# A larger pad at the top of SBUF: right-hand MLP operands 256 bytes off the weights, where they were 128 off

## The chip, the cores and the metric

The kernel runs on one core of one Trainium2 chip. The metric is the device time of one execution in microseconds; less is better. The time before is the median of three runs.

## The reference

One decoder layer on `x` of 1 x 1024 x 1024, all in float32: a mixer block, an MLP block and a final RMSNorm. Cut to what matters here:

```python
for l in range(DEPTH):                                   # DEPTH = 1
    h = rms_norm(x, norm_mix[l])
    x = x + hybrid_mixer(h, ...)                         # 8 projections 1024->1024, RG-LRU, HGRN2, gates, w_out
    h = rms_norm(x, norm_mlp[l])
    x = x + jnp.square(jax.nn.relu(h @ w_up[l])) @ w_down[l]   # 1024 -> 4096 -> 1024
return rms_norm(x, norm_final)
```

The MLP block is where the change acts.

## The kernel before, in words

**How a float32 product is made.** Every large matrix operand is split into a high part (a rounding to TensorE's `fp32r` type) and a low part (what is left), each a tile of its own. `split` writes them, ScalarE the high part (L76) and VectorE the low part (L77). `mm3` then makes one product from three matmuls, L115, L116 and L117:

```python
def mm3(o, ah, al, bh, bl, first, last, goes_on=False):
    PE.matmul(o, ah, bh, start=first, stop=False, **how)    # L115
    PE.matmul(o, ah, bl, start=False, stop=False, **how)    # L116
    PE.matmul(o, al, bh, start=False, stop=last, **how)     # L117
```

The first operand of a matmul (`ah`, `al`) is the one loaded into the array, 128 columns or 512 bytes of a partition; below it is called the loaded operand. The second (`bh`, `bl`) is streamed, 512 columns or 2048 bytes of a partition (256 columns in `pv` alone); below it is called the streamed operand. Each matmul has a weight load of its own, and TensorE loads the operand of the next matmul while the present one streams.

**The stages.** First the mixer, in two halves of the sequence: projections (`pj_*`, `pv`), the recurrences, gates, and the output projection (`po`). Then the second norm, made while the second half's output projection runs. Then the *up* stage (`hidden`, matmuls `uX`, `uY`, `uZ`), 16 quads of hidden channels with a seven-product scheme (`PLAN`): 16 x 7 x 4 x 3 = 1344 matmuls of 512 columns. Its squared-ReLU results are split and, for 14 of 16 quads, written to DRAM. Last the *down* stage (`dX`, `dY`, `dZ`), eight blocks of two quads each, again 1344 matmuls, added into `acc` by VectorE (L963), then the final norm and the output. The scheduler's order on every engine is fixed when the kernel is built.

**Where the operands lie.** Tiles are taken from a stack that grows from the left (low addresses) and one that grows from the right (the top of SBUF, downward). On the left lie, among others, the raw and split weights (`wp`: `wH`, `wL`, `ws..`, `wA..`; `w1`), the mixer's activations (`a2h`: `hT`, `a2y`: `y`), and the first set of MLP hidden operands (`ust`: `u0..`, `u2..`). All of these start at 256 past a multiple of 512 bytes. On the right lie the up stage's streamed operands (`h2..`), and in the down stage a second set of everything (`late_u`, `late_w`, `late_w1`, `late_raw`) and the sums `acc`. Ahead of all of these stands a tile that nobody uses:

```python
pad, close_pad = opened("pad", side="right")
pad.tile([P, 24], F32, tag="pad", name="pad")            # 96 bytes of a partition
h2p = [opened(f"h2{i}", side="right") for i in range(4)]
```

All tiles behind it are multiples of 512 bytes long, so the pad alone sets where each of them starts, modulo 512: before, at 384. Within the tiles every slice that a matmul of these stages takes starts at a multiple of 512 bytes. So, modulo 512:

| | loaded operand | streamed operand |
|---|---|---|
| projections `pj`, output projection `po` | 256 (`wH`, `wL`) or 256 (`y`) | 256 (`hT`) or 256 (`wH`, `wL`) |
| up stage `uX`, `uY`, `uZ` | 256 (`ws`, `wA`) | 384 (`h2..`) |
| down stage, first quad of a block | 256 (`ust`) | 256 (`wp`, `w1`) |
| down stage, second quad of a block | 384 (`late_u`) | 384 (`late_w`, `late_w1`) |

In the down stage the two quads take turns:

```python
for i, q in enumerate(qs):                               # i = 0: left tiles, i = 1: right tiles
    for pr in prs:
        mm3(banks[bk, pr], uh[:, cut], ul[:, cut], wh, wl, ...)
```

With two `pr` that is six matmuls with left tiles, then six with right tiles. So at the last matmul of each six the streamed operand lies on one side, and the next operand, loaded meanwhile, on the other.

Of the kernel before, what the change touches and what calls it, by code (L numbers as in the profile page):

```python
# [10 lines left out]
F32 = mybir.dt.float32  # L11
# [7 lines left out]
P = 128  # L19
# [22 lines left out]
def trunk(ctx: ExitStack, tc: tile.TileContext, x, wts, mlp, pv, gains, mask_f, mask_u, out):  # L42
# [8 lines left out]
    def opened(name, **how):  # L51
        cm = tc.tile_pool(name=name, bufs=1, reuse_waits="tile", **how)
        return cm.__enter__(), lambda: cm.__exit__(None, None, None)
# [617 lines left out]


    pad, close_pad = opened("pad", side="right")
    pad.tile([P, 24], F32, tag="pad", name="pad")

    h2p = [opened(f"h2{i}", side="right") for i in range(4)]
    HOME = {"T4": 0, "B22": 0, "T3": 0, "B21": 1, "n2": 2, "t1": 2, "B11": 3}
# [371 lines left out]
```

## Time and profile before

| | |
|---|---|
| median of 3 runs | 1626.46 us (1626.07 to 1626.98) |
| the profiled execution, its own time | 1627.6 us |
| its span, first to last instruction | 1625.8 us |
| mean granted TensorE clock | 0.996 |
| up stage, first to last matmul in the trace | about 987 to 1309 us |
| down stage | about 1304 to 1618 us |

The time differs from the span by 1.8 us, which lies outside the instructions. "Busy" counts an engine's instructions, without waits. A matmul's record is longer than the time until the next one starts, since matmuls overlap in the array: a record of 0.39 us stands in a row of starts that are 0.23 us apart. The pace of TensorE is therefore read from the starts, or from a stretch of time over the number of matmuls in it. Releasers (what ended a wait) are inferred.

### The profile page before, as it was taken

Reading aid. Unit: us, or ns where it says so; the run is one execution under the profiler, and the core shown is the slowest. Engines: PE = TensorE matmul, PEld = TensorE weight load, DVE = VectorE, ACT = ScalarE, POOL = GpSimd, SP = SyncE. Lnnn points to the kernel's source line nnn. Section 1 sums busy time; section 2 is a strip of 40 time slices with the busy share of each in tenths; the row PEclk is TensorE's granted clock in tenths of the full one; section 3 lists DMA queues with packets and bytes.
Section 4 is the critical chain, followed back from the end, with each engine's and each line's share of the span. In section 5 each row is a group of like instructions: output and inputs, shape, how many; then the busy total and the mean of one; then the engine's idle time right before and its main releaser. Section 6 shows DMA issues by size and latency. Waiting matters only on the chain.

```text
span 1625.8 us, 23177 instructions
## 1 busy us (share of the span) xinstructions
PE 1583.0 (97%) x9240; PEld 1306.5 (80%) x9240; DVE 1212.2 (75%) x1751; ACT 764.6 (47%) x1186; POOL 65.0 (4%) x99
## 2 busy tenths in 40 slices
PE   7999999999999999999999997999999999999998
PEld 6788788788788788788787876888888877888886
DVE  5975956848764865848759688977777888788876
ACT  4643545435442544436434566766776732222113
POOL 0010100100100000000100100000000000000000
PEclk9999999999999999999999998999999999999999
DMA  6212212122243222222122362666656575666652
GB/s 237 91 66 91 92 66 104 66 91 92 79 167 135 86 78 90 80 78 103 67 91 91 117 207 104 248 248 250 237 233 246 223 269 213 256 255 247 256 209 104
DMA packets 57996, 246.51 MB, mean 152 GB/s; under 512 B 6688, under 2 KB 6816, under 8 KB 47136
## 3 DMA queue, kind: packets, MB, share of 16 engines
q1 hardware_dynamic: 56304, 239.27, 39.4%
q10 hardware_dynamic: 1584, 5.77, 1.0%
q8 instruction: 72, 1.18, 0.3%
q14 instruction: 36, 0.29, 0.1%
HBM read 185.24 MB, written 59.77 MB: 151 GB/s over the span
## 4 chain that ended last, share of the span: by engine, by line
PE 80%; DVE 15%; DMA 2%; issue 1%; ACT 1%; POOL 0%; DVEq 0%; POOLq 0%; SPq 0%; ACTq 0%
PE uX L115 3%; PE uX L117 3%; PE dX L115 3%; PE uX L116 3%; PE dX L117 3%; PE dX L116 3%; DVE wL L77 2%; PE pj_ga L117 2%; PE pv L116 2%; PE pv L117 2%; PE pv L115 2%; PE pj_ga L115 2%; PE pj_ga L116 2%; PE pj_f L117 2%; PE pj_ma L115 2%; PE pj_ma L117 2%
## 5 line engine op out<-in xcount | busy, mean ns | idle before, releaser
L77 DVE TENSOR_TENSOR wL<-raw,wH 128x1024 fp32r<-128x1024 f32 x160 | 194.3, 1214 | 150.0 <-ACT wH L76 145.8
L76 ACT CAST wH<-raw 128x1024 fp32r<-128x1024 f32 x160 | 167.8, 1049 | 166.3 <-issue 66.4
L963 DVE TENSOR_TENSOR acc<-acc,dX 128x512 f32<-128x512 f32 x128 | 85.1, 682 | 30.4 <-PE dX L117 29.7
L76 ACT CAST wA<-q 128x512 fp32r<-128x512 f32 x32 | 19.8, 621 | 129.0 <-PE dX L117 102.1
L963 DVE TENSOR_TENSOR acc<-acc,dY 128x512 f32<-128x512 f32 x64 | 43.5, 685 | 16.0 <-PE dY L117 15.1
L345 DVE RECIPROCAL rr<-rr 128x512 f32<-128x512 f32 x16 | 53.5, 3346 | 0.0
L823 ACT ACTIVATE b<-b 128x512 f32<-128x512 f32 x48 | 30.2, 631 | 38.4 <-DVE b L822 38.3
L115 PE MATMUL pv<-wH,hT0H 128*128 128x256 f32 x128 | 37.7, 294 | 0.0
L116 PE MATMUL pv<-wL,hT0H 128*128 128x256 f32 x128 | 37.4, 293 | 0.0
L117 PE MATMUL pv<-wH,hT0L 128*128 128x256 f32 x128 | 37.4, 292 | 0.0
L115 PE MATMUL pv<-wH,hT1H 128*128 128x256 f32 x128 | 36.5, 285 | 0.0
L116 PE MATMUL pv<-wL,hT1H 128*128 128x256 f32 x128 | 36.2, 283 | 0.0
L117 PE MATMUL pv<-wH,hT1L 128*128 128x256 f32 x128 | 36.2, 283 | 0.0
L311 DVE SCALAR_TENSOR_TENSOR xc<-xp,pvt,xc 128x512 f32<-128x512 f32 x48 | 33.1, 746 | 0.0
L551 ACT ACTIVATE on<-po 128x128 f32<-128x128 f32 x64 | 17.0, 278 | 33.4 <-PE po L541 33.2
L570 ACT ACTIVATE smb<-pj_mb 128x512 f32<-128x512 f32 x16 | 9.6, 597 | 45.4 <-PE pj_mb L117 45.2
L824 ACT ACTIVATE b<-b 128x512 f32<-128x512 f32 x48 | 30.0, 630 | 1.1
L77 DVE TENSOR_TENSOR wA<-q,wA 128x512 fp32r<-128x512 f32 x32 | 21.9, 686 | 10.5 <-ACT wA L76 10.3
L565 ACT ACTIVATE g<-pj_g 128x512 f32<-128x512 f32 x16 | 9.6, 599 | 37.3 <-PE pj_g L117 37.3
L444 POOL TENSOR_SCALAR seg<-seg 128x128 f32<-128x128 f32 (+1 forms) x16 | 12.7, 792 | 360.4 <-DVE seg L384 360.4
L384 DVE TENSOR_TENSOR seg<-seg 128x128 f32<-128x128 f32 (+2 forms) x96 | 26.7, 305 | 0.2
L117 PE MATMUL pj_ga<-hT1H,wL 128*128 128x512 f32 x64 | 26.5, 414 | 0.0
(1854 smaller groups left out, 5264.3 us busy)
## 6 DMA issues: line engine op xcount, KB each, us to landing
raw<-wts_in SPq DMA_DIRECT2D x160, 512.0 KB, 3.4
q<-mlp_in SPq DMA_DIRECT2D x64, 512.0 KB, 4.0
x<-x_in SPq DMA_DIRECT2D x8, 512.0 KB, 5.8
acc<-x ACTq DMA_DIRECT2D x8, 512.0 KB, 6.5
y_out<-acc SPq DMA_DIRECT2D x16, 256.0 KB, 2.1
xs<-x_in SPq DMA_DIRECT2D x8, 256.0 KB, 3.3
x<-xs SPq DMA_DIRECT2D x8, 256.0 KB, 2.4
x2s<-x_in SPq DMA_DIRECT2D x4, 512.0 KB, 4.4
```

What stands on the lines that cost most here:

```text
L76: keep(A.copy(h, src))
L77: keep(V.tensor_tensor(out=lo, in0=src, in1=h.bitcast(F32), op=ALU.subtract))
L115: PE.matmul(o, ah, bh, start=first, stop=False, **how)
L116: PE.matmul(o, ah, bl, start=False, stop=False, **how)
L117: PE.matmul(o, al, bh, start=False, stop=last, **how)
L311: V.scalar_tensor_tensor(xc[:, s, :], xp[:, j : j + T], pvt[:, PV_CW + 8 * j + u : PV_CW + 8 * j + u + 1], xc[:, s, :], op0=ALU.mult, op1= ...
L345: V.reciprocal(rec, rec)
L384: mul = lambda o, a, b: V.tensor_tensor(out=o, in0=a, in1=b, op=ALU.mult)
L551: A.activation(on[:, 4 * s + n, :], po[:, n * P : (n + 1) * P], AF.Square, accum_out=ssq[:, 4 * s + n : 4 * s + n + 1])
L823: A.activation(b[:, at, :], b[:, at, :], AF.Relu, scale=-1.0 if at == 2 else 1.0)
L824: A.activation(b[:, at, :], b[:, at, :], AF.Square)
L963: V.tensor_tensor(out=dst, in0=dst, in1=banks[bk, pr], op=op)
```

## The change

The unused tile at the top of SBUF is 480 bytes of a partition long in place of 96. Every tile of the right-hand stack that comes after it (`h2..`, `late_u`, `late_w`, `late_w1`, `late_raw`, `acc`) lies 384 bytes lower, and so starts at a multiple of 512 bytes, where it started at 384 past one. Nothing on the left moves, and the instructions, their order and their waits stay the same on every engine.

```diff
     pad, close_pad = opened("pad", side="right")
-    pad.tile([P, 24], F32, tag="pad", name="pad")
+    pad.tile([P, 120], F32, tag="pad", name="pad")
 
     h2p = [opened(f"h2{i}", side="right") for i in range(4)]
```

In the table above each 384 becomes 0 (or 512); the 256 stay.

## The prediction

> **What bounds the kernel now.** I read the page first, for the bound; then the starts of matmuls in three stages, for TensorE's pace; then who makes TensorE wait in the two stages that the change touches.
>
> ```profile
> span 1625.8 us, 23177 instructions
> PE 1583.0 (97%) x9240; PEld 1306.5 (80%) x9240; DVE 1212.2 (75%) x1751; ACT 764.6 (47%) x1186; POOL 65.0 (4%) x99
> PE 80%; DVE 15%; DMA 2%; issue 1%; ACT 1%; POOL 0%; DVEq 0%; POOLq 0%; SPq 0%; ACTq 0%
> 1100.00:1200.00 100.00, 100.00 (x431) 80.31 (x430) 78.98 (x97) 69.63 (x97) 0.00 (x0) 1.00 0.61 237
> 1400.00:1500.00 100.00, 100.00 (x440) 82.54 (x439) 78.68 (x113) 20.16 (x22) 0.00 (x0) 1.00 0.57 226
> PE uX L115 <- ACT ws30H L76: 1.7, 1, 1.7
> PE uZ L115 <- ACT braw L705: 0.5, 1, 0.5
> PE dZ L116 <- DVE wA1230L L77: 1.1, 1, 1.1
> PE dX L115 <- DVE acc L963: 1.1, 3, 0.4
> ```
>
> The last six rows are two stretches of the view by windows (busy time and count of TensorE, its weight loads, VectorE, ScalarE, GpSimd; then granted clock, share of the DMA engines, GB/s) and all that the view of waits lists for TensorE from 990 us to the end; the row above them is the chain that ended last, four fifths of it TensorE. In the up stage (1100 to 1200) and the down stage (1400 to 1500) TensorE is busy all the time at full clock, VectorE under 80%, and in 636 us it waits 4.4 us. So there the time is the number of matmuls times the distance of their starts, and only what alters that distance counts.
>
> That distance is not the same everywhere. Here are the first and last row of three unbroken stretches of TensorE's instructions in order of time (start, us, line, out<-streamed,loaded for `pj` and `u`): 84 rows of a projection, 100 of the up stage, 103 of the down stage.
>
> ```profile
> 644.77 0.39 PE L115 MATMUL pj_f<-hT1H,wH 128*128 128x512 f32 x1
> ...
> 663.58 0.39 PE L117 MATMUL pj_g<-hT1H,wL 128*128 128x512 f32 x1
> 1134.82 0.40 PE L117 MATMUL uY<-h2t1H,ws17L 128*128 128x512 f32 x1
> ...
> 1157.92 0.39 PE L117 MATMUL uX<-h2n2H,ws18L 128*128 128x512 f32 x1
> 1469.71 0.39 PE L117 MATMUL dX<-ws122H,u6n 128*128 128x512 f32 x1
> ...
> 1492.98 0.39 PE L117 MATMUL dZ<-wA1223H,u7B 128*128 128x512 f32 x1
> ```
>
> Projection: (663.58 - 644.77) / 83 steps = 226.6 ns. Up stage: (1157.92 - 1134.82) / 99 = 233.3 ns here, and over the longer window 100 us / (431 - 1.7) = 232.9 ns (a record of 0.39 us begins up to 1.7 steps before the window and is counted in it). Down stage: (1492.98 - 1469.71) / 102 = 228.1 ns. Same kind of matmul, same shape, same clock. In the table of addresses they differ in one thing: in the projection the streamed operand and the operand being loaded have the same place modulo 512, in the up stage they lie 128 apart, in the down stage 128 apart once in six matmuls.
>
> That it is the address and not the stage is seen at the turns of the down stage:
>
> ```profile
> 1440.25 0.40 PE L117 MATMUL dY<-ws320H,u4B 128*128 128x512 f32 x1
> 1440.48 0.39 PE L115 MATMUL dY<-ws321H,u5B 128*128 128x512 f32 x1
> 1440.71 0.39 PE L116 MATMUL dY<-ws321L,u5B 128*128 128x512 f32 x1
> 1440.94 0.39 PE L117 MATMUL dY<-ws321H,u5B 128*128 128x512 f32 x1
> 1441.17 0.39 PE L115 MATMUL dY<-ws321H,u5B 128*128 128x512 f32 x1
> 1441.39 0.39 PE L116 MATMUL dY<-ws321L,u5B 128*128 128x512 f32 x1
> 1441.62 0.40 PE L117 MATMUL dY<-ws321H,u5B 128*128 128x512 f32 x1
> ```
>
> The two matmuls of 0.40 us, first and last, are the ones that stream from one side while the next operand is loaded from the other; the five between, with both on the right, are shorter. And it does not matter which way: in the first the streamed operand lies at 256 and the loaded one at 384, in the last at 384 and 256. A loss that is the same at +128 and at -128 is the second fact on which I build.
>
> **The change, part by part.** *The up stage.* The offset between streamed and loaded goes from 128 to 256 (modulo 512) for 1344 matmuls. No matmul of 512 columns in this trace has that offset, so its price is bounded from both sides. From below, the best pace in the trace, 226.6 ns at offset 0: a gain of 232.9 - 226.6 = 6.3 ns a matmul. From above, a loss that grows with the distance: offset 128 costs 6.3 ns over offset 0, so 256 would cost 12.6, that is 6.3 ns more than now. The middle is the same price as now.
>
> I take the lower end. If two streams disturb each other by meeting in the same part of a memory that repeats every 512 bytes, one that runs ahead by 128 and one that runs behind by 128 (ahead by 384) meet at different times of the load, and I'd expect different losses. If the pattern repeats every 256 bytes, +128 and -128 are the same offset, as the two equal rows have it. Then 256 is the same as 0. One other place has an offset of 256, in matmuls of 128 columns in the mixer (`sn` at 384 is streamed while `scT` at 128 is loaded; `v` at 128 while `qf` at 256):
>
> ```profile
> 425.49 0.38 PE L541 MATMUL po<-sn,qf 128*128 128x128 f32 x2
> 425.71 0.39 PE L538 MATMUL po<-v,scT 128*128 128x128 f32 x2
> 425.93 0.39 PE L541 MATMUL po<-sn,qf 128*128 128x128 f32 x2
> 426.15 0.39 PE L538 MATMUL po<-v,scT 128*128 128x128 f32 x2
> ```
>
> Each pair starts 0.22 us after the one before, whether it ends with an offset of 256 (L541) or of 128 (L538). So 256 brings no loss of its own there; but 128 brings none either, so this speaks only weakly.
>
> Some 1300 of the 1344 matmuls gain, since the first dozens wait for others (the two `ws30H` and `braw` rows above). 1300 x 6.3 ns = 8.2 us. Nothing else holds that stage: VectorE has 79 us of work in 100 us, and it would have it in 97.3. Only the stage's end is different, as the chain that ended last shows:
>
> ```profile
> 1286.95 1.05 ACT wA1215H L76
> ...
> 1303.64 4.62 DMA q<-mlp_in
> ...
> 1311.72 1.15 DVE wA1230L L77
> 1312.91 0.50 PE dZ L116
> ```
>
> From 1287 to 1313 it runs through ScalarE, VectorE and a load of weights and not through TensorE. What TensorE gains in those 26 us, 26 x 6.3 / 232.9 = 0.7 us, it waits out at `dZ` L116, on top of the 1.1 us there now. Left of the up stage: 7.5 us.
>
> *The down stage.* Within a quad both operands move together or neither moves: no change. At the turns the offset goes from 128 to 256, in both directions. By the paces above the turns now cost 228.1 - 226.6 = 1.5 ns a matmul on average, 1344 x 1.5 = 2.0 us. If 256 is as 0, that goes; TensorE waits for little there, so I count 1.9 us of it.
>
> *Everything else on the right.* VectorE and ScalarE read and write there, and DMAs land there. VectorE shows no price for an offset: the split into `h2T3L` reads one operand at 256 and one at 384, that into `wA` two at 256:
>
> ```profile
> L77 DVE TENSOR_TENSOR h2T3L<-braw,h2T3H 128x512 fp32r<-128x512 f32 x2 | 1.4, 688 | 0.0
> L77 DVE TENSOR_TENSOR wA<-q,wA 128x512 fp32r<-128x512 f32 x17 | 11.6, 685 | 0.2
> ```
>
> 3 ns either way on the few hundred VectorE instructions of these stages is under 1 us, and it lies under TensorE with a fifth of VectorE's time free; without that cover it would be that 1 us. DMAs into right-hand tiles are covered the same way: of the waits in the down stage none is long and only the chain above has a load in it. I count nothing for both.
>
> Sum: 7.5 + 1.9 = 9.4 us. The profiled execution took 1627.6 us (span 1625.8), so it would take 1618.2; the median of the runs is 1.1 us lower, which gives 1626.5 - 9.4 = 1617.1 us.
>
> **The rule that speaks against it.** TensorE's pace depends on where the operands lie, 226.6 against 232.9 ns. The Trainium skill, "TensorE: Matmul & The Clock Gate", Part 2 (what happens when a matmul is issued), has two independent SBUF read ports in TensorE, and says that loading the next tile's weights takes no read bandwidth from the running matmul. By that rule no offset would matter, and the time would stay at 1626.5 us. The two paces above don't agree with it, as long as nothing but the offset tells the stages apart; the 0.40 us rows inside one stage are my reason to think so.
>
> **The rivals.** *Not faster, not slower.* A load and a stream may disturb each other once for every time that one overtakes the other, at a fixed price whenever that falls inside the load, so that only offset 0, where they start together, escapes. Equal rows at +128 and -128 fit this too. Then 256 costs what 128 costs: 1626.5 us. The case in which offsets mean nothing at all, and the stages differ by something that I haven't seen, ends at the same time. Against both: a meeting early and a meeting late in the load should leave a different rest of the load to suffer.
>
> *Slower.* The loss grows with the distance, and 256, half way round 512, is the farthest that two operands can be apart: the meeting falls in the middle of the load, where most of it is still to come or just done. It also is the same at +128 and -128, so the two rows can't exclude it. Priced linearly: 1300 x 6.3 = 8.2 us in the up stage, 2.0 us at the turns, 1636.7 us. It decides once the up stage's starts are more than 235.3 ns apart: 0.2% of the time is 3.25 us, over 1344 matmuls 2.4 ns each, on 232.9.
>
> *Part of the gain.* 256 is better than 128 but not as good as 0, or the end of the up stage and the first loads of the down stage hold back more than 0.7 us: half the sum, 1621.8 us.
>
> **How the numbers follow.** About 0.2%, 3.25 us, is what a measurement of this kernel can tell from no change. Faster as summed: 0.51; part of it: 0.08; no change: 0.15; slower: 0.26. So faster 0.59, same 0.15, slower 0.26. The likeliest case's own range is 1615 (the whole 8.5 us of 1344 matmuls, the turns, and 1 us for matmuls that may go below 226.6) to 1620. Cases of both signs hold most of the chance, so the full range runs from 1614 past no change into the slower case, up to 1634, three quarters of its linear price; its far end, and the little below 1614, are left out with less than 2 in 10.
>
> **What would show it.** In the profile after: starts in the up stage 226.6 to 227.5 ns apart, that is 441 to 443 matmuls in a window of 100 us in which 431 stood; no 0.40 us rows at the turns of the down stage, and 442 or 443 there in place of 440; the wait at `dZ` L116 grown from 1.1 to about 1.8 us; projections and everything before 980 us as before; VectorE's 688 and 685 ns unchanged. I am wrong if the up stage keeps 431 (rival of no change) or shows under 427 (slower), and wrong in the reason if the time falls elsewhere.

## The result: 0.41% faster

| | median | runs |
|---|---|---|
| before | 1626.35 us | 6 (1625.81 to 1627.95) |
| after | 1619.25 us | 6 (1618.30 to 1622.63) |

The ratio is 0.9959, with a 95% interval of 0.9946 to 0.9972: 6.7 us, between 4.6 and 8.8. The profiled execution after took 1621.54 us with a span of 1619.7, 6.1 us under the span before. The forecast was 1617.1 us.

The page after; the view by windows for TensorE alone (window, length, busy time and count, clock, DMA share, GB/s); and, in order of time, the first and the last of 103 unbroken rows of the up stage and of 104 of the down stage:

```profile
span 1619.7 us, 23177 instructions
PE 1574.4 (97%) x9240; PEld 1304.5 (81%) x9240; DVE 1211.2 (75%) x1751; ACT 763.1 (47%) x1186; POOL 64.9 (4%) x99
PE 77%; DVE 17%; DMA 2%; issue 2%; ACT 1%; POOL 0%; DVEq 0%; POOLq 0%; SPq 0%; ACTq 0%
```

```profile
1100.00:1200.00 100.00, 99.66 (x438) 1.00 0.62 240
1210.00:1280.00 70.00, 70.00 (x309) 1.00 0.64 248
1510.00:1600.00 90.00, 90.00 (x398) 1.00 0.44 174
```

```profile
1134.69 0.39 PE L115 MATMUL uY<-h2t1H,ws17H 128*128 128x512 f32 x1
...
1157.81 0.39 PE L115 MATMUL uZ<-h2B21H,wA128H 128*128 128x512 f32 x1
...
1469.42 0.39 PE L117 MATMUL dZ<-wA1223H,u7B 128*128 128x512 f32 x1
...
1492.77 0.39 PE L115 MATMUL dY<-ws323H,u7B 128*128 128x512 f32 x1
```

Up stage: 23.12 us / 102 steps = 226.7 ns, where it was 233.3. Down stage: 23.35 / 103 = 226.7 ns, where it was 228.1. Both now have the projection's pace. The turns of the down stage, which stood out with 0.40 us, are gone. The rows below pass from the left tiles (`u4B`) to the right ones (`u5B`) between 1440.86 and 1441.09:

```profile
1440.63 0.39 PE L116 MATMUL dX<-wA,u4B 128*128 128x512 f32 x1
1440.86 0.39 PE L117 MATMUL dX<-wA,u4B 128*128 128x512 f32 x1
1441.09 0.39 PE L115 MATMUL dX<-wA,u5B 128*128 128x512 f32 x1
```

So in unbroken rows every matmul got what was forecast. The window from 1100 to 1200 us holds 438 matmuls all the same, and not the 441 to 443 of the forecast, because TensorE pauses in it. Here is all that the view of waits lists for TensorE from 985 to 1310 us, the second norm's (`xT_h`) left out:

```profile
PE uX L115 <- ACT ws30H L76: 2.0, 1, 2.0
PE uZ L115 <- ACT braw L705: 1.1, 1, 1.1
PE dZ L116 <- DVE wA1230L L77: 0.9, 1, 0.9
PE uX L117 <- DVE wA L77: 0.5, 1, 0.5
...
PE uX L115 <- ACT e L819: 0.3, 1, 0.3
```

Before, the first two were 1.7 and 0.5 us, and the last two weren't there; the one at `dZ`, which lies behind 1310 us there, was 1.1. In the up stage proper TensorE waits 3.9 us where it waited 2.2. Not all of these waits cost time; the part on the sum below says which do.

### The profile page after: what moved, and what is told of

Same layout as the page of the kernel before. It is cut to its first block, busy times and chain, and to the rows that moved or that the text cites. A ratio compares the mean times of both kernels' runs of the same rounds, so it can differ in the third digit from the quotient of the medians.

```text
span 1619.7 us, 23177 instructions
## 1 busy us (share of the span) xinstructions
PE 1574.4 (97%) x9240; PEld 1304.5 (81%) x9240; DVE 1211.2 (75%) x1751; ACT 763.1 (47%) x1186; POOL 64.9 (4%) x99
## 4 chain that ended last, share of the span: by engine, by line
PE 77%; DVE 17%; DMA 2%; issue 2%; ACT 1%; POOL 0%; DVEq 0%; POOLq 0%; SPq 0%; ACTq 0%
PE dX L115 3%; PE dX L116 3%; PE dX L117 3%; PE uX L115 3%; PE uX L117 3%; PE uX L116 3%; DVE wL L77 2%; PE pj_ga L117 2%; PE pv L116 2%; PE pv L117 2%; PE pv L115 2%; PE pj_ga L116 2%; PE pj_ga L115 2%; PE pj_f L117 2%; PE pj_ma L117 2%; PE pj_ma L116 2%
## 5 line engine op out<-in xcount | busy, mean ns | idle before, releaser
L116 PE MATMUL pv<-wL,hT0H 128*128 128x256 f32 x128 | 37.5, 293 | 0.0
L116 PE MATMUL pv<-wL,hT1H 128*128 128x256 f32 x128 | 36.2, 283 | 0.0
```

## The experiments

Two theories stood against each other at first. Mine: the price of an offset between streamed and loaded operand repeats every 256 bytes. The rivals: it grows with the distance, or only offset 0 escapes; or what counts is an address by itself, not the offset. The runs below change a pad and nothing else. For each I show the two windows that measure the pace: with c matmuls in 70 us of the up stage a step is 70 / (c - 1.7), with c in 90 us of the down stage 90 / (c - 1.7). Short pauses in a window are counted in. One matmul more or less is 0.8 and 0.6 ns. Before the change they hold:

```profile
1210.00:1280.00 70.00, 70.00 (x302) 1.00 0.60 234
1510.00:1600.00 90.00, 90.00 (x396) 1.00 0.46 181
```

That is 233.1 and 228.3 ns. After it (309 and 398, above) 227.8 and 227.1 ns. The up stage's 227.8 has two short gaps in it, at an operand `ws3..` of every second quad.

### Offset 0

```diff
-    pad.tile([P, 24], F32, tag="pad", name="pad")
+    pad.tile([P, 56], F32, tag="pad", name="pad")
```

> Pad of 224 bytes: the right-hand operands at 256 modulo 512, as the weights, offset 0. If the pattern repeats every 256 bytes, offset 0 is as 256: up stage 226.6 to 227.1 ns from start to start, time 1618 to 1620 us, as with the pad of 480. If the loss grows with the distance up to some point and 256 is merely a better place than 128, offset 0 is better still: up stage under 226 ns, 1617 us or less. If 256 is a place of its own and 0 is not, up stage near 230 ns, over 1622 us.

```profile
1210.00:1280.00 70.00, 70.00 (x309) 1.00 0.67 257
1510.00:1600.00 90.00, 90.00 (x398) 1.00 0.44 172
```

1618.73 us, ratio 0.9949 (0.9934 to 0.9963). The same counts as with offset 256, to the matmul. The first theory holds so far; 256 is no mere way-point between 128 and something better.

### Offset -128

```diff
-    pad.tile([P, 24], F32, tag="pad", name="pad")
+    pad.tile([P, 88], F32, tag="pad", name="pad")
```

> Pad of 352 bytes: the right-hand operands at 128 modulo 512, 128 below the weights in place of above. If the pattern repeats every 256 bytes, -128 is the same offset as +128: up stage 232.8 ns, turns of the down stage costing 1.5 ns a matmul, 1626.4 us as before. If what counts is which stream is ahead, the up stage has another pace, under 230 or over 236 ns, and the time is more than 3 us away from before.

```profile
1210.00:1280.00 70.00, 70.00 (x302) 1.00 0.61 233
1510.00:1600.00 90.00, 90.00 (x396) 1.00 0.48 189
```

1627.04 us, ratio 1.0001 (0.9991 to 1.0010). Again the counts of +128 exactly. What the turns of the down stage hinted at holds over the whole up stage.

### The weights moved in place of the operands

```diff
+    const.tile([P, 32], F32, tag="padl", name="padl")
     ident = const.tile([P, P], F32, tag="ident", name="ident")
```

This stands on the kernel before, with its pad of 96 bytes; the unused tile comes ahead of `ident`.

> Pad of 96 bytes on the right as before, and an unused tile of 128 bytes at the bottom on the left, so that the weights and all else on the left lie at 384 modulo 512, as the right does: the streamed operands of the up stage keep their addresses modulo 512, and the offset becomes 0. If the offset between the two counts, up stage 227 ns, turns at the common pace, 1618 to 1620 us. If it is the address of the right-hand tiles by itself that counts (384 bad, 0, 256 and the like good), nothing is gained: 232.8 ns, 1626.5 us, and the mixer, whose operands now lie at 384 too, gets slower than 226.6 ns as well.

```profile
1210.00:1280.00 70.00, 70.00 (x309) 1.00 0.67 257
1510.00:1600.00 90.00, 90.00 (x398) 1.00 0.44 172
```

1619.46 us, ratio 0.9953 (0.9935 to 0.9971). The right-hand tiles lie where they lay before, at 384, and the gain is there all the same; with the larger pad the weights lay where they lay before, at 256, and it was there too. So it is the offset between the two operands, and not where either lies.

### The up stage alone, and the down stage alone

```diff
+    pad2, close_pad2 = opened("pad2", side="right")
+    pad2.tile([P, 32], F32, tag="pad2", name="pad2")
     late_u, close_late_u = opened("late_u", side="right")
```

That is the up stage alone, on the kernel after; `pad2` is also closed at the end with the other tiles. The down stage alone has the pad of 96 bytes and `pad2` of `[P, 96]`.

> Pad of 480 bytes for the up stage, and a second pad of 128 bytes that puts everything of the down stage on the right back to 384 modulo 512, as before. By the prediction's terms the up stage keeps its gain and the turns of the down stage lose theirs: up stage 227.0 ns, down stage 228.1 ns, about 2 us slower than the pad of 480 alone (1620.5 to 1621.5 us). If the down stage's gain came from something else on the right (landing DMAs, VectorE), it goes too, and the matmuls with both operands on one side would be seen to change.

> Pad of 96 bytes for the up stage as before, and a second pad of 384 bytes that puts the down stage's right-hand tiles at multiples of 512. The other half of the run with the up stage alone: up stage 232.8 ns as before, turns of the down stage at the common pace, about 2 us under before: 1624 to 1625 us. If the gains of the two stages don't add (the down stage's first loads holding back), it is under 1 us.

Up stage alone:

```profile
1210.00:1280.00 70.00, 70.00 (x309) 1.00 0.65 250
1510.00:1600.00 90.00, 90.00 (x396) 1.00 0.44 172
```

Down stage alone:

```profile
1210.00:1280.00 70.00, 70.00 (x302) 1.00 0.61 233
1510.00:1600.00 90.00, 90.00 (x399) 1.00 0.47 182
```

1620.95 us, ratio 0.9963 (0.9950 to 0.9976), and 1625.50 us, ratio 0.9985 (0.9976 to 0.9995). Each stage keeps its own pace, gained or not, whatever the other does. The two gains, 6.0 and 2.4 us by the ratios, add up to 8.4, which the whole change's own interval of 4.6 to 8.8 us holds. The down stage has only its turns to gain from, so these are worth about 2 us, as summed.

### Smaller offsets: +64, -64, -32, +32

```diff
-    pad.tile([P, 24], F32, tag="pad", name="pad")
+    pad.tile([P, 40], F32, tag="pad", name="pad")
```

That is offset 64. `[P, 8]` gives 192, `[P, 128]` 224 and `[P, 48]` 32. By a period of 256 bytes 192 is -64 and 224 is -32.

> Pad of 160 bytes: offset 64. If a loss rises smoothly from offset 0 to its height at 128, 64 lies between: up stage about 230 ns, 1622 us. If two streams disturb each other wherever they are not exactly in step (offset 0 modulo 256), 64 costs what 128 costs: 232 to 234 ns, 1626 us. If parts of memory of 128 bytes take turns, 64 is half in the same part and half in the next, 228 to 232 ns.

> Pad of 32 bytes: offset 192, which by a period of 256 is -64. The run at +64 had 229.1 ns in the up stage and 230.7 ns within the quads of the down stage, 1626.0 us in all; at its turns the streams at -64 were followed by starts 227.2 ns apart, those at +64 by 230.9. If the sign counts below 128, the up stage at -64 is faster than at +64: 226 to 228 ns. If it is only the distance, 229 ns. The whole then 1618 to 1626 us, since the turns of the down stage have both signs in either case.

> Pad of 512 bytes, which modulo 512 is no pad at all: offset 224, by a period of 256 that is -32. If the loss is smooth round 0, under 1 ns a matmul: 1619 to 1621 us. If any step out of a common multiple of 128 or 64 costs, 229 ns and more, 1622 to 1628 us.

> Pad of 192 bytes: offset +32, the mirror of the run at 224 (-32), which had 233.3 ns in the up stage. If the sign counts as it does at 64 (229.1 ns at +64, 233.3 at -64), +32 lies well below 233, 227 to 230 ns. If only in step (0 modulo 256) is free and +64 is the exception, 232 to 234 ns. The whole 1622 to 1628 us, since the turns of the down stage have both signs.

Offset 64:

```profile
1210.00:1280.00 70.00, 70.00 (x306) 1.00 0.63 242
1510.00:1600.00 90.00, 90.00 (x392) 1.00 0.44 175
```

Offset 192, or -64:

```profile
1210.00:1280.00 70.00, 70.00 (x302) 1.00 0.61 233
1510.00:1600.00 90.00, 90.00 (x393) 1.00 0.47 185
```

Offset 224, or -32 (modulo 512 the place that the tiles have without a pad):

```profile
1210.00:1280.00 70.00, 70.00 (x301) 1.00 0.61 233
1510.00:1600.00 90.00, 90.00 (x393) 1.00 0.47 184
```

Offset 32:

```profile
1210.00:1280.00 70.00, 70.00 (x301) 1.00 0.60 232
1510.00:1600.00 90.00, 90.00 (x393) 1.00 0.46 180
```

| offset | up stage, ns | down stage, ns | median, us | ratio (interval) |
|---|---|---|---|---|
| +64 | 230.0 | 230.6 | 1625.98 | 0.9992 (0.9982 to 1.0001) |
| -64 | 233.1 | 230.0 | 1629.64 | 1.0019 (1.0010 to 1.0029) |
| -32 | 233.9 | 230.0 | 1629.10 | 1.0008 (0.9999 to 1.0018) |
| +32 | 233.9 | 230.0 | 1629.27 | 1.0012 (1.0003 to 1.0021) |

Here my expectations mostly missed. At +64 the up stage came out half way, as a smooth curve would have it, but the time didn't. At -64 I had read from a few turns that it would be fast, and it is as slow as 128: what follows a single turn doesn't tell the pace of a row of such matmuls. At 32, either way, the loss is as large as at 128. So the price is no smooth function of the distance. Of the eight offsets tried it is gone only at 0 and 256; +64 is the one place between.

The down stage shows a second thing. Within a quad both operands lie alike, and still it runs at 230.0 to 230.6 ns with turns of 32 or 64, slower than with turns of 128 (228.3). At offset 64 the records show where:

```profile
1441.56 0.40 PE L117 MATMUL dX<-wA1221H,u5t 128*128 128x512 f32 x1
1441.79 0.40 PE L115 MATMUL dX<-wA1221H,u5t 128*128 128x512 f32 x1
1442.03 0.39 PE L116 MATMUL dX<-wA1221L,u5t 128*128 128x512 f32 x1
1442.25 0.39 PE L117 MATMUL dX<-wA1221H,u5t 128*128 128x512 f32 x1
1442.48 0.39 PE L115 MATMUL dX<-wA,u4B 128*128 128x512 f32 x1
1442.71 0.40 PE L116 MATMUL dX<-wA,u4B 128*128 128x512 f32 x1
```

The turns are at 1442.25 and, ahead of these rows, at 1440.88. The long records are the third and fourth matmul after the one and the second after the other, among operands that are in step. It is no chance of these rows: over the 82 unbroken groups of six that follow a turn like the first of these, the third and the fourth matmul take 233.1 and 235.5 ns to the next start. So the loss doesn't stay with the matmul at the turn. The kernel before has a little of it too: 232.5 ns at the turn and 230.6 at the matmul behind it, and 226 to 227 at the other four.

### Offsets 256 and 0, side by side

The two kernels of before, unchanged, in five rounds on one chip.

> The changed kernel itself once more (pad of 480, offset 256), beside the pad of 224 (offset 0) on the same chip. If the two offsets are one and the same, the medians lie within 1 us of each other, near 1619 us, and the up stage runs at 227.0 ns in both. The 2 us that were short of the forecast: if they go to a stretch of half clock after the first wait of the up stage that some executions have and some have not, single times fall into two groups about 1.6 us and more apart, the lower near 1618.3.

> Pad of 224 bytes (offset 0) again, beside the pad of 480. Same as the pad of 480 if the period is 256: within 1 us. If 256 has a price of its own that its profile hid (the mean of the starts is then over 0.4 ns apart), this one is faster by 1 us or more.

Offset 256: 1619.34 us (1617.76 to 1620.91), ratio 0.9950 (0.9937 to 0.9962). Offset 0: 1618.96 us (1618.29 to 1619.86), ratio 0.9948 (0.9935 to 0.9960). They are the same within what can be told; no version of these beats the changed kernel. The two groups of times that I expected don't show: 1617.76, 1619.09, 1619.34, 1619.95 and 1620.91 lie too evenly. But the first profile of the changed kernel has a stretch of half clock in this window, and this second one has not. Window 1005 to 1020 us (TensorE, its weight loads, VectorE, ScalarE, GpSimd, clock, DMA) and some rows in it, the first execution:

```profile
1005.00:1020.00 15.00, 12.97 (x49) 9.92 (x48) 7.29 (x11) 7.93 (x14) 0.00 (x0) 0.89 0.19 70
```

```profile
1010.33 0.50 PE L115 MATMUL uX<-h2T3H,ws30H 128*128 128x512 f32 x1 [1.97 <-ACT ws30H L76]
...
1013.23 0.63 PE L115 MATMUL uX<-h2T3H,ws30H 128*128 128x512 f32 x1
1013.65 0.63 PE L116 MATMUL uX<-h2T3L,ws30H 128*128 128x512 f32 x1
1014.08 0.63 PE L117 MATMUL uX<-h2T3H,ws30L 128*128 128x512 f32 x1
```

and the second:

```profile
1005.00:1020.00 15.00, 12.98 (x57) 10.08 (x56) 8.90 (x13) 9.49 (x17) 0.00 (x0) 1.00 0.19 70
```

In the first, eight matmuls after the 2 us wait start 0.43 us apart in place of 0.23, at a mean clock of 0.89 over the window. That is 8 x 0.20 = 1.6 us, and the two profiled executions are 1621.54 and 1619.09 us long. From 1011.9 to 1015.3 us the granted clock is 0.50 in the first and 1.00 in the second. The same stretch stands in five of the 13 profiles: with the up stage in step (this one and the up stage alone) and out of step (offsets 64 and -128, the down stage alone). So the change doesn't bring it about.

## Why the prediction was right

**The bound and the pace.** Right: starts 226.7 ns apart in both stages, 226.6 was the forecast.

**The price of 256.** Right, and for the reason given: 0 and 256 are one offset, +128 and -128 another, in whole stages and not only at the turns. The rival in which only offset 0 escapes needed 302 matmuls in the window and there are 309. The rival in which the loss grows with the distance falls with 32, which costs as much as 128, and with 256, which costs nothing. Some luck was in it: the step from two equal rows at the turns to a period of 256 is the kind of reading that failed at -64. And what it is that repeats every 256 bytes stays open; the runs show the price, not its cause.

**The rule on the read ports.** The Trainium skill, "TensorE: Matmul & The Clock Gate", Part 2, says that loading the next tile's weights takes no read bandwidth from the running matmul. Taken as a rule that the place of the weights costs a matmul nothing, it doesn't hold here: 128 bytes of unused tile under the weights changed 302 matmuls in 70 us to 309. Whether read bandwidth is what is lost, no run here shows.

**The sum.** Here terms were mis-sized, 9.4 us against 6.7 and (second measurement, by its ratio) 8.1.

*The up stage*, 7.5 us forecast, ran from 987.05 to 1309.05 us before and from 987.76 to 1305.46 after: 4.3 us. The first matmul that needs `ws30H` started 22.57 us after the stage's first, before and after alike: ScalarE and VectorE set that stretch. It holds 72 matmuls, of which I had left out 44, and the longer wait for `braw` and the new one for `wA` (at 993.51 us) lie in it and cost nothing. Behind it are 1271 steps. By the unbroken ones, 232.8 ns before and 227.0 after, they gained 7.4 us. The half clock took 1.6 of that (before, there is such a stretch too, from 988 to 991 us, but it lies in the first 22.57 us and cost nothing; so it is in the second profile of the changed kernel, whose up stage is 316.05 us long and gained 5.95). Pauses where `uX` comes to `ws3..H`, in eight of the quads from `ws31H` to `ws315H`, took the other 1.5: they add up to 1.8 us, and before to 0.3. The longest is at `ws310H`: ScalarE's copy `e` (L819) reads `uX` out, and TensorE writes it again only then. The weight load (PEld) waited 0.22 us for it before and 0.77 after:

```profile
1200.84 0.19 PEld L115 LDWEIGHTS uX<-h2T3H,ws310H 128*128 128x128 f32 x1 [0.22 <-ACT e L819]
1199.30 0.19 PEld L115 LDWEIGHTS uX<-h2T3H,ws310H 128*128 128x128 f32 x1 [0.77 <-ACT e L819]
```

I had charged 0.7 us for the stage's end alone and taken ScalarE and VectorE for free elsewhere, by VectorE's share of 79% in the middle of the stage. But they work in order, and where a single operand or a free accumulator is due a faster TensorE only arrives earlier.

*The wait at `dZ` L116* was to grow to 1.8 us and shrank to 0.9. This is the chain after:

```profile
1279.00 0.70 DVE b L822
...
1281.02 0.95 ACT ws315H L76
...
1300.28 3.54 DMA q<-mlp_in
...
1307.90 1.15 DVE wA1230L L77
1309.09 0.50 PE dZ L116
```

It leaves TensorE at 1279 us, 30 us ahead of `dZ`, where it was 26. But it isn't of fixed length, as I had assumed. Before, VectorE stood still for 0.38 us at L759 until the load that the chain passes through had landed; after, the load is there in time:

```profile
1308.62 0.69 DVE L759 TENSOR_TENSOR s<-q,q 128x512 f32<-128x512 f32 x1 [0.38 <-DVE s L759]
1304.20 1.29 DVE L759 TENSOR_TENSOR s<-q,q 128x512 f32<-128x512 f32 x2
```

The view names L759, an instruction of VectorE itself, as the releaser; that it was the load is read from the chain before, where the load ends at 1308.26. What the rest of the chain gained I have not worked out.

*The down stage*, 1.9 us forecast for the turns: from its first to its last matmul 314.2 us before and 311.6 after, 2.6 us; with the other half undone the turns alone gave 1.6 us by the medians, 2.4 by the ratio.

**Start of the up stage.** It began 0.7 us later after the change, though nothing ahead of it on TensorE had moved in step. With that, 4.3 + 2.6 - 0.7 = 6.2 us, against the span's 6.1. In the six profiles with the up stage in step it began between 987.60 and 987.76 us, in the seven others between 986.11 and 987.27. I can't say what sets it; whether the addresses cost time there too stays open.

**VectorE.** Indifferent, as assumed: the split of one operand at 256 and one at 384 took 688 ns before; with the second at 0 it takes 689.

## What to carry to other kernels

Where TensorE is the bound and its matmuls follow each other without a gap, compare the distance of their starts between stages of the same shape. A few per cent of the pace (here 226.7 ns against 233.3) can lie in nothing but the addresses of the two operands, and a pad takes them back: here streamed and loaded operand are to start at the same place modulo 256 bytes. And read the gain of a faster bound against the single operands that are due, not against the other engines' shares.

## What the runs showed of the hardware

- A matmul of 512 columns of `fp32r` with a load of 128 columns beside it: 226.7 ns from start to start in unbroken rows with streamed and loaded operand at an offset of 0 or 256 bytes. By the window in the up stage, pauses counted in, 227.8 ns at 0 and 256, 233 to 234 at 32, 128, 192 (-64), 224 (-32) and -128, 230 at +64.
- The offset counts at the turn from one operand to the next, and a turn of 32 or 64 slows matmuls that follow it: 230.0 to 230.6 ns in a stage where five in six matmuls are in step.
- Matmuls of 128 columns in `fp32` show no such price: single ones started 111 to 112 ns apart at offsets of 0, 128 and 256 alike, between 425.7 and 426.4 us of the trace before (the pairs shown ahead of the forecast each hold two offsets, so by themselves they don't tell).
- After a wait of 2.0 us eight matmuls in a row started 0.43 us apart, in one execution of a program and not in another; in all, in five of 13 profiles, after waits of 1.7 to 2.0 us, and in the other eight not, after waits of the same length. The Trainium skill, "TensorE: Matmul & The Clock Gate", Part 1, has a gate that halves the clock after idleness and looks at windows of about 3.4 us; the stretch here is 8 x 0.43 = 3.4 us long, which agrees. The wait ahead of it was shorter than such a window.
